# Moving four gate pairs of a hybrid mLSTM/HGRN step between its HGRN heads, parking their sums in DRAM, and another lead-in

## The chip, the cores and the metric

The kernel runs on one core of one Trainium2 chip. The metric is the device time of one execution in microseconds; the time of a kernel is the median of its runs. Everything below is fp32 work; every dense product is carried out as three TensorE passes over parts that are rounded to the fp32r format.

## The reference, cut to what matters

```python
xn = rmsnorm(h, norm_g)
proj = xn @ w_in
u, v_m, z_m, ig, fg, q_h, f_h, i_h, g_h, ga, gb = split(proj)
# branch a: causal conv, 4 mLSTM heads of 512, chunk by chunk
ya = hm @ w_brm
# branch b: 8 HGRN2 heads of 128
lfh = log(lb + (1 - lb) * sigmoid(f_h));  kh = (1 - lb) * sigmoid(-f_h);  qh = silu(q_h)
oh, S_new = hgrn(qh, kh, i_h, lfh, S0)
yb = (head_rmsnorm(oh, hnorm_g) * silu(g_h)) @ w_brh
y = sigmoid(ga) * ya + sigmoid(gb) * yb
h = h + y @ w_out
h = h + sigmoid(h @ w_pg) * (p @ w_ple)
out = rmsnorm(h, final_g)
```

There are 512 prompt frames of a new stream and 32 frames of a running one, a model width of 1024, one layer. The outputs are y for both streams and all new states (conv rows, C, n, m, S). `ga` and `gb` are 1024 wide each, that is 8 units of 128 columns each.

## The kernel before

**Tiles.** The 544 frames lie along the free axis, features along the 128 partitions. A product over 1024 features has 8 slices; for each slice and each half of the frames (272 columns) there are three matmuls: high weight by high x, high weight by low x, low weight by high x. A weight piece of 128x512 comes by DMA into one of 8 raw buffers (`raw_piece`, L122), ScalarE casts it to the high part (L134) and VectorE subtracts to get the low part (L135). So a dense stretch of TensorE has a steady stream of casts, subtractions and PSUM evacuations beside it on ScalarE and VectorE.

**Order.** TensorE's order is written by hand (`tc.manual_schedule`). The other engines run their queues first in, first out; what stands where in them is decided when the program is built, by a priority. In the lead-in (L1392 on) ScalarE and VectorE are also in written order.

**Lead-in.** VectorE sets a tile `warm` to zero (L1396), TensorE runs 8 dummy fp32 matmuls on it (L1399; each shows as two in the trace), then `products(k)` (L1405) for the 8 slices of the first three units. For each slice x is scaled by the norm's gain on ScalarE (L1413, the high part `hi`), VectorE makes its low part (L1414), and the weight piece `wf` is split as above. All loads are issued on SP's queue, x and wf in turn (L205, L124).

**Middle.** Then come the convolution, the four mLSTM heads and the sum over them of `ya` in DRAM (`ya_d`, L1349 to L1360).

**HGRN part.** `units()` (L1692) is a list of pairs of units (`Two`, L479): for each head h the pair (q, f), then (g, i), and after all eight heads four pairs of `ga` and four of `gb` in turn. A pair is computed with seven blocks of 12 matmuls each in place of eight (the sums of weights for it are made by DMA with accumulate and by VectorE), so it takes 14 steps of 6 matmuls. `Pump` (L704) hands these steps to TensorE one by one; `heads()` (L2035) is a generator with the recurrence of the heads: it issues some small TensorE work of a head and what follows it on the other engines, and then yields a number of steps for which the pump runs before the next piece of the chain. These numbers are `GAPS` (L40). The pieces of a head that matter here, by the names of their PSUM tiles:

- `ho` (`output`, L2007): the head's output; then on ScalarE sums of squares, on VectorE a Newton reciprocal root on 128x5 tiles and the scaling of `kq` by it (L2026)
- `hoT` (`finish`, L2098), `GAPS[10]`, `[2]`, `[3]` and `[4]` later, 12 steps in all: transposes of the scaled output back to features by frames; VectorE gates it into `ob` (L2107, L2108)
- `pl` (`scores`): the attention scores of the levels of the recurrence
- `ht` (`columns`, L1819): transposes of `hkq` (the keys) and of `hi` (the values), evacuated by ScalarE (L1822, L1823)
- `su` (`state`, L1988): the state's update from these, `GAPS[8]` steps behind `ht`

`merge_a` (L1747) is run when a `ga` unit is there: sigmoid on ScalarE, `ya` loaded from `ya_d`, VectorE multiplies (L1751), and the product stays in a slot `ya` until the end. `merge_b` (L1754) takes the sigmoid of `gb`. After the last head's `hoT` the pump runs out, with gate pairs alone.

**Seam and end.** Then `p @ w_ple` (tiles `ple`), `yb` (L2194 on): each of the 8 `ob` tiles is split into high and low part (`os`), each unit's 48 matmuls are followed by times `gb`, plus `yas[f]`; then the pairs of `w_out` and `w_pg`, and the final norm.

Of the kernel before, what the change touches and what calls it, by code (L numbers as in the profile page):

```python
# [17 lines left out]
P = 128  # L18
# [9 lines left out]
HH = 8  # L28
# [9 lines left out]
SUB = 5  # L38
LASTS = (0, 3, 6)
GAPS = (2, 2, 1, 3, 6, 2, 4, 2, 2, 4, 2, 8)  # L40
SLOT = 550
NSLOT = 22
NEVAC = 12
# [26 lines left out]
def hybrid_step(ctx: ExitStack, tc: tile.TileContext, a, o):  # L70
# [48 lines left out]
        V.tensor_tensor(lo, src, hi.bitcast(F32), ALU.subtract)  # L119
        return hi, lo  # L120

    def raw_piece(src, name):  # L122
        raw = wp.tile([P, WP], F32, tag="wr", name=name, bufs=NRAW)
        nc.sync.dma_start(raw[:, : src.shape[-1]], src)  # L124
        return raw

    made = {}
# [75 lines left out]
    def load(k):  # L203
        t = eslot(f"x{k}")
        nc.sync.dma_start(t[:, : T + 1], a["xT"][k])  # L205
# [1186 lines left out]

    with tc.manual_schedule(engines={mybir.EngineType.Activation, mybir.EngineType.DVE, mybir.EngineType.PE}):

        warm = small("warm", [P, P], bufs=1, tag="vsm")
        V.memset(warm, 0.0)  # L1396
        wps = paux("warm")
        for _ in range(WARM):
            PE.matmul(wps[:, 0, :P], warm, warm, start=True, stop=True)  # L1399
# [3 lines left out]
        acc.append([u2[:, 0], u2[:, 1]])  # L1403

        def products(k):  # L1405
            for f in range(NF):
                steps(acc[f], wf[k][1:], (k,), f * P, 0)

        for k in range(KD):
            t = xt[k]  # L1410
            hi, lo = pair_tile(f"x0{k}", k // (KD // 2))
            g = t[:, T : T + 1]
            S.mul(hi, t[:, :T], g)  # L1413
            V.scalar_tensor_tensor(lo, t[:, :T], g, hi.bitcast(F32), ALU.mult, ALU.subtract)  # L1414
            x0.append((hi, lo))
            wf[k].append(split_piece(wf[k][0], f"wf{k}", NF * P))
            if k == 1:
                load(KD - 2)
                load(KD - 1)
            sqk = slot(f"r0q{k}")[:, :T]  # L1420
            S.activation(sqk, t[:, :T], AF.Square)
            sq.append(sqk)
            if k in (1, 3):
                V.tensor_tensor(sq[k - 1], sq[k - 1], sqk, ALU.add)
            if k in (5, 6):
                i, j = ((0, 2), (4, 5))[k - 5]
                V.tensor_tensor(sq[i], sq[i], sq[j], ALU.add)
            if k > 1:
                products(k - 2)
# [260 lines left out]
    gbs, yas, gated = [None] * KD, [None] * KD, {}  # L1690

    def units():  # L1692


        def both(h):

            if "both" not in hs[h]:
                t = sp.tile([P, 2, SLOT], F32, tag="d", name=f"hkq{h}", bufs=2)
                hs[h].update(both=(t[:, 0], t[:, 1]), pair=t)
            return hs[h]["both"]  # L1700

        def forget(h, raw):
            lbc, lcc = lb[:, h : h + 1], lc[:, h : h + 1]
            tf, kk = eslot(f"tf{h}"), both(h)[0]
            for t, sign in ((tf, 1.0), (kk, -1.0)):
                S.activation(unrev(t), raw[:, :HB], AF.Sigmoid, scale=sign)
                S.activation(t[:, HB:T], raw[:, HB:T], AF.Sigmoid, scale=sign)
            S.activation(tf[:, :T], tf[:, :T], AF.Identity, scale=lcc, bias=lbc)
            S.mul(kk[:, :T], kk[:, :T], lcc)
            hs[h].update(tf=tf, kk=kk, kq=raw)  # L1710

        def query(h, qq):
            tf, kk, kq = (hs[h][k] for k in ("tf", "kk", "kq"))
            q0 = eslot(f"q0{h}")

            S.activation(unrev(q0), qq[:, :HB], AF.Sigmoid)
            S.activation(q0[:, HB:T], qq[:, HB:T], AF.Sigmoid)
            V.tensor_tensor(unrev(q0), unrev(q0), qq[:, :HB], ALU.mult)
            V.tensor_tensor(q0[:, HB:T], q0[:, HB:T], qq[:, HB:T], ALU.mult)
            V.tensor_tensor(qq[:, :T], q0[:, :T], tf[:, :T], ALU.mult)  # L1720
            hs[h].update(q0=q0, qq=qq)

        def behind(h, then, t):

            if h:
# [12 lines left out]
        def value(h, t):
            hs[h]["ii"] = t

        def gate(h, t):
            sg = slot(f"sg{h}")
            S.activation(sg[:, :T], t[:, :T], AF.Sigmoid)
            V.tensor_tensor(t[:, :T], t[:, :T], sg[:, :T], ALU.mult)
            hs[h]["gg"] = t

        def merge_a(f, t):  # L1747
            gated[f] = S.activation(t[:, :T], t[:, :T], AF.Sigmoid)
            y = slot(f"ya{f}")[:, :T]
            nc.sync.dma_start(y, ya_d[f])  # L1750
            V.tensor_tensor(y, y, t[:, :T], ALU.mult)  # L1751
            yas[f] = y

        def merge_b(f, t):  # L1754
            S.activation(t[:, :T], t[:, :T], AF.Sigmoid)
            gbs[f] = t

        for h in range(HH):
# [22 lines left out]
        for f in range(0, KD, 2):  # L1781
            for e in (
                pair("ga", f, 80 + f, lambda f: plain(eslot(f"ga{f}")), merge_a, True),
                pair("gb", f, 88 + f, lambda f: plain(eslot(f"gb{f}")), merge_b, True),
            ):
                e.alone = True
                yield e

    def triangle(out, x, sign):

# [244 lines left out]
    def heads():  # L2035
# [7 lines left out]
        x.collect()  # L2043
        x.copies(1)
        for h in range(HH):
            yield max(1, pump.when["i", h] - pump.done)
            x.scale(1)
            x.copies(2)
            yield GAPS[1]
            if last:  # L2050
                last.output()
                yield GAPS[10]
            x.values()
            yield GAPS[2]
            x.scale(2)
            x.copies(3)
            x.shares()
            yield GAPS[3]
# [4 lines left out]
            yield GAPS[4]  # L2063
            if last:
                finish(h - 1)
            x.scale(4)
            x.copies(5)
            yield GAPS[5]
            x.scale(5)
            x.copies(6)  # L2070
            nxt = None
            if h + 1 < HH:
                yield max(1, pump.when["q", h + 1] + 1 - pump.done)
                nxt = Head(h + 1)
                nxt.copies(0)
                yield GAPS[6]
            else:
                yield GAPS[11]
# [11 lines left out]
            yield GAPS[7]  # L2090
            x.columns(x.kk, x.kt, x.kts)
            yield GAPS[8]
            x.state()
            last, x = x, nxt
        yield GAPS[9]
        last.output()

    def finish(h):  # L2098
# [14 lines left out]
    with tc.manual_schedule(engines={mybir.EngineType.PE}):  # L2113
# [17 lines left out]
    ps_, ple = [], []  # L2131
    for k in range(2):
        t = slot(f"p{k}")
        nc.sync.dma_start(t[:, :T], a["pT"][k])
        with tc.issue_after(gated[KD // 2 + k].ins):
            ps_.append(split(t[:, :T], f"ps{k}"))

    def ple_units(n, after=None):
        for f in range(len(ple), len(ple) + n):
# [54 lines left out]
    for f in (0, 4, 1, 5, 2, 6, 3, 7):  # L2194
        w = weight(a["w_brh"][f], f"wbh{f}")
        acc = dense(w, 0, P, P, obs, f"yb{f}")
        t = gbs[f]
        for b in range(2):
# [220 lines left out]
```

## Time and profile before

| | us |
|---|---|
| runs: median (lowest to highest of 3) | 1091.33 (1090.9 to 1091.63) |
| the profiled execution, its own time | 1091.98 |
| its span | 1090.0 |
| TensorE busy in it | 1080.7 |
| VectorE busy | 897.3 |
| ScalarE busy | 700.3 |
| GpSimd busy | 217.2 |

A row of the timeline reads: start in us, duration in us, engine, line, operation, output<-inputs by tile name, shape, count; in brackets the idle time before it and what ended it. `PE` is the matmul, `PEld` the load of its weights, which goes ahead of it. Because a matmul's modelled end overlaps the start of the next (0.29 us long, but one starts every 0.125 us), a short wait hardly shows as idle time: it is seen as a larger distance between two starts, and the matmul behind it shows 0.39 in place of 0.29.

### The profile page before, as it was taken

Reading aid. Unit: us, or ns where it says so; the run is one execution under the profiler, and the core shown is the slowest. Engines: PE = TensorE matmul, PEld = TensorE weight load, DVE = VectorE, ACT = ScalarE, POOL = GpSimd, SP = SyncE. Lnnn points to the kernel's source line nnn. Section 1 sums busy time; section 2 is a strip of 40 time slices with the busy share of each in tenths; the row PEclk is TensorE's granted clock in tenths of the full one; section 3 lists DMA queues with packets and bytes.
Section 4 is the critical chain, followed back from the end, with each engine's and each line's share of the span. In section 5 each row is a group of like instructions: output and inputs, shape, how many; then the busy total and the mean of one; then the engine's idle time right before and its main releaser. Section 6 shows DMA issues by size and latency. Waiting matters only on the chain.

```text
span 1090.0 us, 26205 instructions
## 1 busy us (share of the span) xinstructions
PE 1080.7 (99%) x9865; PEld 1054.9 (97%) x9865; DVE 897.3 (82%) x2052; ACT 700.3 (64%) x1619; POOL 217.2 (20%) x399
## 2 busy tenths in 40 slices
PE   9999999999999999999999999999999999999998
PEld 9899999999999999999999999999999999999997
DVE  6889988676897695986888689999999887778886
ACT  7767557754666564765556488778777667446673
POOL 5205010213021122202130033223332210000002
PEclk9999999999999999999999999999999999999999
DMA  6134525648454377555599666667666783327753
GB/s 233 58 117 136 182 66 168 156 136 207 137 170 151 125 169 171 170 171 176 178 257 246 192 147 153 153 145 156 151 155 145 184 224 98 115 89 242 237 195 122
DMA packets 97270, 176.67 MB, mean 162 GB/s; under 512 B 11412, under 2 KB 18580, under 8 KB 96888
## 3 DMA queue, kind: packets, MB, share of 16 engines
q1 hardware_dynamic: 81072, 140.96, 40.1%
q0 software_dynamic: 15184, 32.93, 16.5%
q8 instruction: 77, 1.26, 0.5%
q10 hardware_dynamic: 888, 1.12, 0.3%
q14 instruction: 49, 0.40, 0.1%
HBM read 150.05 MB, written 41.69 MB: 176 GB/s over the span
## 4 chain that ended last, share of the span: by engine, by line
PE 79%; DVE 10%; ACT 6%; DMA 3%; issue 2%; SPq 0%; ACTq 0%; DVEq 0%
PE d L610 33%; PE ya L169 9%; PE yb L169 4%; PE q L169 4%; PE k L169 4%; PE C L1079 4%; PE sc L1039 2%; PE u L293 2%; PE d L462 2%; PE vp L1572 2%; PE nm L1260 2%; DVE hkq L1936 1%; PE ple L169 1%; DMA ws<-in_w_in 1%; DMA kv_d<-vhl 1%
## 5 line engine op out<-in xcount | busy, mean ns | idle before, releaser
L497 POOL DMA_DIRECT2D ws<-in_w_in x46 | 40.3, 883 | 208.8 <-DVE hkq L1936 79.8
L624 ACT COPY t<-d 128x272 f32<-128x272 f32 x153 | 57.9, 378 | 13.6 <-PE d L610 13.4
L1936 DVE TENSOR_TENSOR hkq<-hkq,q 128x288 f32<-128x288 f32 (+1 forms) x96 | 41.8, 437 | 4.4 <-ACT km L1858 3.6
L787 DVE SCALAR_TENSOR_TENSOR cv<-ub,vec,cv 128x547 f32<-128x547 f32 x48 | 37.6, 784 | 1.7 <-ACT cv L782 1.2
L1193 DVE SCALAR_TENSOR_TENSOR c<-c,wi,Cs 128x258 f32<-128x258 f32 x32 | 15.3, 479 | 18.8 <-PE Cs L1191 18.6
L1357 DVE TENSOR_TENSOR y<-ya,y 128x272 f32<-128x272 f32 x48 | 18.9, 435 | 14.3 <-PE ya L169 12.5
L1091 ACT COPY Co<-C 128x258 f32<-128x258 f32 x30 | 9.8, 378 | 27.1 <-PE C L1079 24.8
L779 POOL COPY uo<-ub 128x3 f32<-128x3 f32 x16 | 18.7, 1167 | 34.5 <-DVE ub L633 26.6
L963 POOL COPY ksm<-kf 128x96 f32<-128x96 f32 x16 | 8.1, 510 | 84.8 <-ACT kf L977 84.8
L135 POOL TENSOR_TENSOR wple50l<-wple5r,wple50h 128x256 fp32r<-128x256 f32 x1 | 0.7, 737 | 120.1 <-ACT wple50h L134 120.1
L1271 ACT COPY y<-nm 128x516 f32<-128x516 f32 x16 | 9.5, 591 | 23.0 <-PE nm L1260 22.5
L963 POOL COPY vsm<-vt 128x96 f32<-128x96 f32 x12 | 6.3, 526 | 85.9 <-ACT vt L635 43.5
L1248 DVE BATCH_NORM_STATS2 bs<-y 128x6 f32<-128x512 f32 (+1 forms) x20 | 13.8, 691 | 8.1 <-ACT y L1271 7.8
L583 POOL DMA_DIRECT2D ws<-in_w_in x14 | 14.3, 1023 | 29.8 <-DVE ws272l L135 26.6
L1260 PE MATMUL nm<-vhl,sh 128*128 128x258 f32 x112 | 18.4, 286 | 0.0
L378 POOL DMA_DIRECT2D w_pg_d<-in_w_pg x16 | 13.1, 820 | 25.3 <-issue 22.1
L1977 POOL COPY at<-at 32x128 f32<-32x128 f32 x32 | 17.9, 558 | 1.4 <-ACT at L1958 0.4
L2022 ACT ACTIVATE kit<-kq 128x128 f32<-128x128 f32 x32 | 9.7, 304 | 12.0 <-DVE kq L2018 12.0
L1008 DVE TENSOR_TENSOR ql<-q,qh 128x272 fp32r<-128x272 f32 x24 | 9.4, 434 | 8.3 <-ACT qh L1007 7.2
L378 POOL DMA_DIRECT2D w_out_d<-in_w_out x16 | 13.5, 1005 | 12.7 <-issue 10.6
L1260 PEld LDWEIGHTS nm<-vhl,sh 128*128 128x128 f32 x112 | 15.5, 190 | 0.6 <-ACT Co L1091 0.5
L1792 POOL TENSOR_SCALAR_AFFINE_SELECT aa<-at 128x128 f32<-128x128 f32 x32 | 15.7, 523 | 0.6
(4748 smaller groups left out, 5112.5 us busy)
## 6 DMA issues: line engine op xcount, KB each, us to landing
ws<-in_w_in POOLq DMA_DIRECT2D x60, 256.0 KB, 5.1
ws<-in_w_in SPq DMA_DIRECT2D x46, 256.0 KB, 4.0
ya_d<-y SPq DMA_DIRECT2D x32, 272.0 KB, 2.3
y<-ya_d SPq DMA_DIRECT2D x24, 272.0 KB, 3.6
w_out_d<-in_w_out POOLq DMA_DIRECT2D x24, 256.0 KB, 6.2
w_pg_d<-in_w_pg POOLq DMA_DIRECT2D x24, 256.0 KB, 6.3
c<-in_C SPq DMA_DIRECT2D x16, 258.0 KB, 3.6
out_Cs<-c SPq DMA_DIRECT2D x16, 258.0 KB, 3.7
```

Of the source, the lines that this page charges most:

```text
L169: PE.matmul(both[b][:m, :TH], part(w, off + k * step, m, x), xx[:, half(b)], start=(k == 0 and j == 0), stop=(k == n - 1 and j == 2),)
L293: PE.matmul(both[b][:m, :TH], part(w, off + k * step, m, x), xx[:, half(b)], start=(k == 0 and j == 0), stop=(k == KD - 1 and j == 2),)
L378: G.dma_start(late[g][n][k], src, accum_op=ALU.add)
L462: PE.matmul(self.ps[b][:, : c.stop - c.start], part(self.w, k * P, P, x), xx[:, c], start=(k == 0 and j == 0), stop=(k == KD - 1 and j == 2),)
L497: G.dma_start(t, piece(u, i), accum_op=ALU.add)
L610: PE.matmul(ps, ww[:, c], xx, start=(start and k == 0 and j == 0), stop=end, skip_group_check=not start,)
L624: self.kept = S.copy(t, ps)
L787: V.scalar_tensor_tensor(cv[:, :547], ub[:, j : j + 547], vcol(V_CW + 4 * ft + j), cv[:, :547], ALU.mult, ALU.add)
L1039: PE.matmul(pn[:, 0, :n], ks[f][x][:, j * P : (j + 1) * P], qs[f][y][:, NS + j * P : T], start=(f == 0 and i == 0), stop=(f == KH - 1 and ...
L1079: PE.matmul(pn[g][:, :VH], kw[b][x][:, f * P : (f + 1) * P], vv[b][y][:, g * VH : (g + 1) * VH], start=(b == 0 and j == 0), stop=(b == NB ...
L1260: PE.matmul(pn[:, g, :VH], st[j][x][:, (i - j) * P : (i - j + 1) * P], vv[j][y][:, g * VH : (g + 1) * VH], start=(j == 0 and q == 0), stop ...
L1936: V.tensor_tensor(x, x, d, ALU.mult)
```

## The change

Four parts.

1. **Lead-in.** The dummy matmuls take a constant zero as operand, so that nothing is set by VectorE before them. The first two pieces of `wf` are loaded on ScalarE's queue. For slice 0 VectorE casts the weight, ScalarE scales x in two halves, VectorE makes the low parts by halves, and the low part of the weight comes last; the 18 matmuls of slice 0 go pass by pass over the three units, not unit by unit.
2. **Gate pairs.** The four `ga` pairs are yielded behind heads h = 3, 4, 5, 6 (`SPREAD`), the four `gb` pairs behind head 7.
3. **Gaps.** Heads 3 to 6 take `WIDE`, the last head `LAST`; the last `hoT` follows 14 steps after the chain's end (`LASTGAP`), not 16, which now falls right ahead of the seam.
4. **Parked sums.** `merge_a` stores the product of gate and `ya` back to `ya_d`; the loop over `yb` loads it again as `yg`, two tiles before the first weight and then one unit ahead. The two splits of p are made within the first two `gb` units that are in `PSAT`.

```diff
+LAST = (2, 4, 2, 4, 8, 4, 4, 2, 2, 4, 4, 8)
+WIDE = (2, 4, 4, 6, 8, 4, 4, 2, 2, 4, 4, 8)
+SPREAD = (3, 4, 5, 6)
+LASTGAP = 14
...
-        wf.append([raw_piece(a["w_first"][k], f"wf{k}r")])
+        wf.append([raw_piece(a["w_first"][k], f"wf{k}r", nc.scalar if k < 2 else nc.sync)])
...
-        warm = small("warm", [P, P], bufs=1, tag="vsm")
-        V.memset(warm, 0.0)
+        warm = nc.const_aps.tensor(0.0, [P, P], F32)
...
+            for j, (x, xx) in enumerate(((0, x0[0][0]), (0, x0[0][1]), (1, x0[0][0]))):
+                for f in range(NF):
+                    for b in range(2):
+                        PE.matmul(
...
+                V.tensor_copy(wh, wf[0][0][:, : NF * P])
+                for b in range(2):
+                    S.mul(hi[:, half(b)], t[:, half(b)], g)
...
+                V.tensor_tensor(wl, wf[0][0][:, : NF * P], wh.bitcast(F32), ALU.subtract)
...
             V.tensor_tensor(y, y, t[:, :T], ALU.mult)
-            yas[f] = y
+            nc.sync.dma_start(ya_d[f], y)
...
+            if h in SPREAD:
+                yield next(gates)
+        yield from gates
...
+            gaps = WIDE if h in SPREAD else LAST if h == HH - 1 else GAPS
...
-        pump.to(pump.done + 16)
+        pump.to(pump.done + LASTGAP)
...
+        for g in order[:2] if i == 0 else order[i + 1 : i + 2]:
+            yas[g] = slot(f"yg{g}")[:, :T]
+            nc.sync.dma_start(yas[g], ya_d[g])
```

**How the order moves.** First the lead-in on TensorE, from its first matmul, before (`u0*`, `u1*`, `u2` are the halves of the three units, `x00` is x's slice 0, `wf0h` and `wf0l` the weight's parts):

```order
L1399 MATMUL warm_152<-warm_150 128x128 x8
L293 MATMUL u00_161<-x00_167,wf0h_170 128x272
L293 MATMUL u01_162<-x00_167,wf0h_170 128x272
L293 MATMUL u00_161<-x00_167,wf0h_170 128x272
L293 MATMUL u01_162<-x00_167,wf0h_170 128x272
L293 MATMUL u00_161<-x00_167,wf0l_171 128x272
L293 MATMUL u01_162<-x00_167,wf0l_171 128x272
```

and the same place of the changed kernel:

```order
L1403 MATMUL warm_150<-const-float32-0.0 128x128 x8
L1417 MATMUL u00_159<-x00_165,wf0wh_166 128x272
L1417 MATMUL u01_160<-x00_165,wf0wh_166 128x272
L1417 MATMUL u10_161<-x00_165,wf0wh_166 128x272
L1417 MATMUL u11_162<-x00_165,wf0wh_166 128x272
L1417 MATMUL u2_164<-x00_165,wf0wh_166 128x272 x2
```

The low part of the weight is now first used by the thirteenth matmul, not by the fifth.

The second place is the transposes `hoT` of head 3, on TensorE, before (`wa2253` and `ws453` are weights of pairs' blocks, `d` their PSUM tiles):

```order
L610 MATMUL d530_11102<-xfh3_1326,wa2253h_11304 128x272
L610 MATMUL d530_11102<-xfl3_1327,wa2253h_11304 128x272
L610 MATMUL d530_11102<-xfh3_1326,wa2253l_11305 128x272
L2103 MATMUL hoT3_11442<-anti_123,kq3_10023 128x128 x2
L2103 MATMUL hoT3_11442<-ident_104,kq3_10023 128x128 x2
L2104 MATMUL hoT3_11442<-anti_123,osb_10419 128x128
L610 MATMUL d531_11103<-xh4_886,ws453h_11371 128x272
```

and of the changed kernel:

```order
L615 MATMUL d771_11676<-xh7_912,wa1277h_11634 128x272
L615 MATMUL d771_11676<-xl7_913,wa1277h_11634 128x272
L615 MATMUL d771_11676<-xh7_912,wa1277l_11635 128x272
L2142 MATMUL hoT3_11722<-anti_123,kq3_10023 128x128 x2
L2142 MATMUL hoT3_11722<-ident_104,kq3_10023 128x128 x2
L2143 MATMUL hoT3_11722<-anti_123,osb_10419 128x128
L615 MATMUL d530_11468<-xfh0_1308,wa2253h_11652 128x272
```

`hoT` stands one block earlier in the pair of unit 53, but the blocks of the gate pair lie ahead of it: counted in the two orders, there are 72 dense matmuls between this head's `ho` and its `hoT` before, and 132 now; between `hoT` and the first matmul on the next weight `ws277`, 12 before and 24 now. Between `ht` of the keys and `su` there are 12 in both; between the scores ahead of it and `ht`, 12 in both.

The third place is VectorE's queue at the seam, in the changed kernel (`wbh` are weights of `yb`, `os` low parts of the `ob` tiles, `ob7` the last head's output):

```order
L140 TENSOR_TENSOR wbh00l_14247<-wbh0r0_14242,wbh00h_14246 128x512
L636 TENSOR_TENSOR gb6_13961<-d941_13960,t1694_14097 128x272
L2146 SCALAR_TENSOR_TENSOR ob7_14164<-hoT7_14158,vec_78,hg7_13059 128x512
L2147 SCALAR_TENSOR_TENSOR ob7_14164<-hoT7_14158,vec_78,hg7_13059 128x32
L124 TENSOR_TENSOR os3_14177<-ob3_11728,os3_14177 128x544
L124 TENSOR_TENSOR os4_14180<-ob4_12419,os4_14180 128x544
L124 TENSOR_TENSOR os5_14183<-ob5_13110,os5_14183 128x544
L124 TENSOR_TENSOR os6_14186<-ob6_13742,os6_14186 128x544
L124 TENSOR_TENSOR os7_14189<-ob7_14164,os7_14189 128x544
L140 TENSOR_TENSOR wbh01l_14251<-wbh0r512_14244,wbh01h_14250 128x512
```

Before, the two `ob7` rows stood some 55 rows ahead of `wbh00l`; all else of these rows was there in nearly the same sequence. On SP's queue 14 DMAs come in on balance (8 stores and 8 loads of 272 KB added, 2 weight loads gone to ScalarE's queue); the number of TensorE instructions is the same but for one row that is printed apart.

More of the change, by code (lines that the diff above doesn't have):

```diff
@@ L120, in psplit, with raw_piece @@
         return hi, lo
-    def raw_piece(src, name):
+    def raw_piece(src, name, queue=None):
         raw = wp.tile([P, WP], F32, tag="wr", name=name, bufs=NRAW)
-        nc.sync.dma_start(raw[:, : src.shape[-1]], src)
+        (queue or nc.sync).dma_start(raw[:, : src.shape[-1]], src)
         return raw
@@ L1405, in products @@
         def products(k):
-            for f in range(NF):
-                steps(acc[f], wf[k][1:], (k,), f * P, 0)
+            if k:
+                for f in range(NF):
+                    steps(acc[f], wf[k][1:], (k,), f * P, 0)
+                return
+            for j, (x, xx) in enumerate(((0, x0[0][0]), (0, x0[0][1]), (1, x0[0][0]))):
+                for f in range(NF):
+                    for b in range(2):
+                        PE.matmul(
+                            acc[f][b][:, :TH],
+                            part(wf[0][1:], f * P, P, x),
+                            xx[:, half(b)],
+                            start=(j == 0),
+                            stop=False,
+                        )
         for k in range(KD):
@@ L1412, in hybrid_step @@
             g = t[:, T : T + 1]
-            S.mul(hi, t[:, :T], g)
-            V.scalar_tensor_tensor(lo, t[:, :T], g, hi.bitcast(F32), ALU.mult, ALU.subtract)
             x0.append((hi, lo))
-            wf[k].append(split_piece(wf[k][0], f"wf{k}", NF * P))
+            if k:
+                S.mul(hi, t[:, :T], g)
+                V.scalar_tensor_tensor(lo, t[:, :T], g, hi.bitcast(F32), ALU.mult, ALU.subtract)
+                wf[k].append(split_piece(wf[k][0], f"wf{k}", NF * P))
+            else:
+                first = [wp.tile([P, WP], F32R, tag=tag, name=f"wf0{tag}") for tag in ("wh", "wl")]
+                wh, wl = (x[:, : NF * P] for x in first)
+                V.tensor_copy(wh, wf[0][0][:, : NF * P])
+                for b in range(2):
+                    S.mul(hi[:, half(b)], t[:, half(b)], g)
+                    V.scalar_tensor_tensor(
+                        lo[:, half(b)], t[:, half(b)], g, hi[:, half(b)].bitcast(F32), ALU.mult, ALU.subtract
+                    )
+                V.tensor_tensor(wl, wf[0][0][:, : NF * P], wh.bitcast(F32), ALU.subtract)
+                wf[0].append(first)
             if k == 1:
@@ L1751, in merge_a, with gate_pairs @@
             V.tensor_tensor(y, y, t[:, :T], ALU.mult)
-            yas[f] = y
+            nc.sync.dma_start(ya_d[f], y)
         def merge_b(f, t):
-            S.activation(t[:, :T], t[:, :T], AF.Sigmoid)
+            opened = S.activation(t[:, :T], t[:, :T], AF.Sigmoid)
             gbs[f] = t
+            if f in PSAT:
+                k = len(ps_)
+                x = slot(f"p{k}")
+                nc.sync.dma_start(x[:, :T], a["pT"][k])
+                with tc.issue_after(opened.ins):
+                    ps_.append(split(x[:, :T], f"ps{k}"))
+        def gate_pairs():
+            for what, unit, then in (("ga", 80, merge_a), ("gb", 88, merge_b)):
+                for f in range(0, KD, 2):
+                    e = pair(what, f, unit + f, lambda f, what=what: plain(eslot(f"{what}{f}")), then, True)
+                    e.alone = True
+                    yield e
+        gates = gate_pairs()
         for h in range(HH):
@@ L1780, in units @@
             )
[L1781 to L1787, printed above, removed]
+            if h in SPREAD:
+                yield next(gates)
+        yield from gates
     def triangle(out, x, sign):
@@ L2048, in heads @@
             x.copies(2)
-            yield GAPS[1]
+            yield gaps[1]
             if last:
                 last.output()
-                yield GAPS[10]
+                yield gaps[10]
             x.values()
-            yield GAPS[2]
+            yield gaps[2]
             x.scale(2)
@@ L2057, in heads @@
             x.shares()
-            yield GAPS[3]
+            yield gaps[3]
             x.scores(paux(f"pl{h}8")[:, 0])
@@ L2062, in heads @@
             x.copies(4)
-            yield GAPS[4]
+            yield gaps[4]
             if last:
@@ L2067, in heads @@
             x.copies(5)
-            yield GAPS[5]
+            yield gaps[5]
             x.scale(5)
@@ L2075, in heads @@
                 nxt.copies(0)
-                yield GAPS[6]
+                yield gaps[6]
             else:
-                yield GAPS[11]
+                yield gaps[11]
             pn = paux(f"pl{h}64")
@@ L2089, in heads @@
                 nxt.copies(1)
-            yield GAPS[7]
+            yield gaps[7]
             x.columns(x.kk, x.kt, x.kts)
-            yield GAPS[8]
+            yield gaps[8]
             x.state()
             last, x = x, nxt
-        yield GAPS[9]
+        yield LAST[9]
         last.output()
@@ L2124, in hybrid_step @@
         pump.run(heads())
-        pump.to(pump.done + 16)
+        pump.to(pump.done + LASTGAP)
         finish(HH - 1)
         pump.end()
[L2131 to L2136, printed above, removed]
+    ple = []
     def ple_units(n, after=None):
@@ L2192, in h_sums @@
         hf[k] = half_sums(f"h{k}", h1[k], h1[k + HK], h1s[k], h, l, h6, l6, after)
-    for f in (0, 4, 1, 5, 2, 6, 3, 7):
-        w = weight(a["w_brh"][f], f"wbh{f}")
+    order = (0, 4, 1, 5, 2, 6, 3, 7)
+    for i, f in enumerate(order):
+        for g in order[:2] if i == 0 else order[i + 1 : i + 2]:
+            yas[g] = slot(f"yg{g}")[:, :T]
+            nc.sync.dma_start(yas[g], ya_d[g])
+        with tc.issue_after(pump.todo[-1].kept.ins) if i == 0 else nullcontext():
+            w = weight(a["w_brh"][f], f"wbh{f}")
         acc = dense(w, 0, P, P, obs, f"yb{f}")
```

5 lines of the change are left out of this document (3 added, 2 removed).

## The prediction

> **What bounds the kernel now.** I read the page first (busy time by engine), then the busy time by stretch where the change works, then what the weight loads of TensorE waited for there, then the timeline around each wait.
>
> ```profile
> PE 1080.7 (99%) x9865; PEld 1054.9 (97%) x9865; DVE 897.3 (82%) x2052; ACT 700.3 (64%) x1619; POOL 217.2 (20%) x399
> ...
> 715.00:831.00 116.00, 114.99 (x1600) 110.60 (x1599) 105.67 (x307) 90.04 (x264) 36.79 (x63) 1.00 0.67 148
> ...
> 858.00:926.00 68.00, 68.00 (x543) 67.70 (x542) 52.82 (x104) 45.36 (x98) 9.15 (x14) 1.00 0.61 162
> ```
>
> TensorE (first figure behind the length of a stretch) is the bound everywhere, so only its waits can be won. VectorE (the third) is at 105.67/116 = 91% while heads run, and at 78% where gate pairs run alone. The change mixes the two kinds of work. The waits of the stretch 715 to 930:
>
> ```profile
> PEld ht L1819 <- DVE hkq L1936: 1.3, 5, 0.3
> PEld hoT L2103 <- PE d L610: 1.1, 3, 0.4
> PEld su L1988 <- ACT kit L1823: 0.6, 2, 0.4
> PEld d L610 <- DVE ws276l L135: 0.4, 1, 0.4
> PEld d L610 <- DVE ws288l L135: 0.4, 1, 0.4
> PEld d L610 <- ACT t L624: 0.2, 1, 0.2
> ```
>
> Columns: total us, times, longest. (A row of 1.5 us that names no releaser is left out.) This is 4.0 us, 0.37% of the kernel, and that is nearly all that the moved pairs can bring.
>
> **Gate pairs and gaps: `hoT`.** An undisturbed transpose follows the last dense matmul by 0.15 us, a waiting one by 0.45:
>
> ```profile
> 726.23 0.29 PE L610 MATMUL d<-xfh,wa2252l 128*128 128x272 f32 x1
> 726.38 0.41 PE L2103 MATMUL hoT<-anti,kq 128*128 128x128 f32 x2
> ...
> 755.60 0.29 PE L610 MATMUL d<-xfh,wa2253l 128*128 128x272 f32 x1
> 756.05 0.41 PE L2103 MATMUL hoT<-anti,kq 128*128 128x128 f32 x2 [0.17 <-DVE kq L2026]
> ```
>
> ```profile
> 755.23 0.68 DVE L2026 TENSOR_TENSOR kq<-kq,hr 128x512 f32<-128x512 f32 x1
> ```
>
> So the releaser is `kq` on VectorE, which ends at 755.9, and the row "PE d" in the table above names only what stood ahead. It happens three times (heads 3 to 5), 0.45 - 0.15 = 0.30 at this one, 1.1 us by the table. There are 72 dense matmuls from `ho` to `hoT`; the chain misses this by 0.3 us. The change makes them 132. At 0.125 us each (below) that is 7.5 us more, against an added VectorE load of one gate pair, of which by the last stretch (78%) about 8 us fall in 10.5 us and only a part in this window. I take the whole 1.1 us, at least half of it.
>
> **Behind `hoT`.** VectorE gates the transposes into `ob`, and then only makes the low part of the next weight:
>
> ```profile
> 756.99 0.74 DVE L2107 SCALAR_TENSOR_TENSOR ob<-hoT,vec,hg 128x512 f32<-128x512 f32 x1
> 757.65 0.68 DVE L135 TENSOR_TENSOR ws277l<-ws,ws277h 128x512 fp32r<-128x512 f32 x1
> ```
>
> ```profile
> 728.62 0.29 PE L610 MATMUL d<-xfl,ws276h 128*128 128x272 f32 x1
> 729.06 0.39 PE L610 MATMUL d<-xfh,ws276l 128*128 128x272 f32 x1 [0.15 <-DVE ws276l L135]
> ...
> 758.39 0.39 PE L610 MATMUL d<-xfh,ws277l 128*128 128x272 f32 x1
> 758.62 0.29 PE L610 MATMUL d<-xfh,ws277h 128*128 128x272 f32 x1
> ```
>
> At 729.06 the matmul starts 0.44 behind its neighbour instead of 0.13. At 758.39 the weight was there by a hair (757.65 + 0.68 = 758.33), and still the next start is 0.23 later, not 0.13: a near miss costs 0.10, and shows in no table. Between `hoT` and this weight there will be 24 matmuls, not 12, 1.5 us more than a wait of 0.31. The rows `ws276l` and `ws288l` go: 0.8 us, and some four near misses of 0.1, that is 0.3 to 0.4. I take 1.1 us; the low end is 0.4, one of the two.
>
> **`su` and `ht`.** Both stand as far behind their sources as before (12 matmuls), so nothing in the order frees them.
>
> ```profile
> 826.14 0.25 ACT L1823 COPY kit<-ht 32x128 f32<-32x128 f32 x1
> ```
>
> ```profile
> 825.96 0.29 PE L610 MATMUL d<-xh,wa1280l 128*128 128x272 f32 x1
> 826.44 0.82 PE L1988 MATMUL su<-hi,hkq 128*128 128x128 f32 x5 [0.19 <-ACT kit L1823]
> ```
>
> `su` waited for ScalarE's queue, in two of five heads, so it hangs on what else stands in it. I take half of 0.6. `ht` waits in all five, for VectorE's `hkq`; I take it as staying, with ends at 1.3 won and 0.3 lost. Where a pair moved in, other pieces may turn late (the PSUM copies of the gate pair stand in ScalarE's and VectorE's queues between links of a chain): ends 0 and 1.2 us, and I take 0.3, one wait of the common size for the four heads together.
>
> **Parked sums.** Eight stores and eight loads, 272 KB each; the same transfer in the old direction:
>
> ```profile
> ya<-ya_d SPq DMA_DIRECT2D x8, 272.0 KB, 5.7
> ```
>
> A load lands 5.7 us after issue; `yg` is wanted only behind 48 matmuls of `yb` (6 us) and then once per 6 us. 4.4 MB more over some 200 us are 22 GB/s on top of 148 to 162 in the rows of stretches. Both cost nothing: TensorE's dense work hides them. A store on SP's queue has to wait for VectorE's product, and weight pieces are queued behind it. What covers it is how early these are issued, here the two pieces of unit 90:
>
> ```profile
> L124 SPq DMA_DIRECT2D wi90r<-in_w_in x2: 327/328/328, 829.8 to 832.1; - x2
> L134 ACT CAST wa1190h<-wi90r x1: 613/613/613, 857.4 to 857.4; 128x512 fp32r<-128x512 f32 x1
> ```
>
> They are issued at 829.8 and 832.1, and the first is cast at 857.4, 27 us later. Without that cover each us of delay would be one us of TensorE. Low end 0, high end 0.5.
>
> **The seam.** The last `hoT` now stands 20 `ple` matmuls ahead of `yb`, so `ob7` and its split come into the row of work there.
>
> ```profile
> 922.87 0.39 ACT L635 ACTIVATE gb<-d 128x272 f32<-128x272 f32 x1
> ...
> 928.09 0.64 ACT L134 CAST wbh01h<-wbh0r 128x512 fp32r<-128x512 f32 x1
> ```
>
> ```profile
> 921.90 2.65 DVE L119 TENSOR_TENSOR os<-ob,os 128x544 fp32r<-128x544 f32 x4 [0.50 <-ACT os L118]
> ...
> 928.98 0.69 DVE L135 TENSOR_TENSOR wbh01l<-wbh0r,wbh01h 128x512 fp32r<-128x512 f32 x1
> ```
>
> ScalarE goes from the last `gb` to `wbh01h` in 928.73 - 922.87 = 5.9 us, with the same rows in both orders. TensorE comes to `wbh01h` behind 5 transposes (0.6 us), 20 and 24 matmuls (5.5 us): 6.1 us. VectorE gets `ob7` in addition, 0.74 us by the row behind `hoT` above and a little more for the sample columns, and the end of the last head's root chain ahead of it. The chain has 76 matmuls, 9.5 us, where 72 missed by 0.3 under heavier load. I charge 0.3 us (ends 0 and 2.0).
>
> **The lead-in.**
>
> ```profile
> 0.80 0.39 SPq L205 DMA_DIRECT2D x<-in_xT  x1
> ...
> 1.12 3.78 PE L1399 MATMUL warm<-warm 128*128 128x128 f32 x16 [1.12 <-DVE emc L1242]
> ...
> 3.53 0.75 ACT L1413 ACTIVATE x<-x 128x544 fp32r<-128x544 f32 x1 [1.44 <-DMA x<-in_xT]
> ...
> 4.18 0.49 ACT L134 CAST wf0h<-wf0r 128x384 fp32r<-128x384 f32 x1
> ...
> 5.01 0.55 DVE L135 TENSOR_TENSOR wf0l<-wf0r,wf0h 128x384 fp32r<-128x384 f32 x1
> ```
>
> ```profile
> 4.73 1.28 PE L293 MATMUL u<-x,wf0h 128*128 128x272 f32 x4
> 5.80 0.66 PE L293 MATMUL u<-x,wf0l 128*128 128x272 f32 x2
> 6.25 1.05 PE L293 MATMUL u<-x,wf0h 128*128 128x272 f32 x4
> 7.14 0.42 PE L293 MATMUL u<-x,wf0l 128*128 128x272 f32 x2
> 7.39 0.66 PE L293 MATMUL u<-x,wf0h 128*128 128x272 f32 x4
> ```
>
> The dummies wait for VectorE until 1.12; an engine that waits for nothing starts at 0.80. They may start 0.3 us earlier and end by about 4.45. x is there at 3.53, half of it scaled by 3.9 (half of 0.75); the weight's cast on VectorE, which the trace doesn't show, lies between ScalarE's 0.49 and VectorE's 0.55 for the shape, so 4.1 to 4.7 by where the piece lands. First useful matmul: 4.5 for 4.73. Matmuls start (7.14 - 5.80)/6 = 0.223 apart until about 7.0, and (7.39 - 7.14)/2 = 0.125 behind it. An earlier start is worth 1 - 0.125/0.223 = 0.44 less than itself: 0.23 x 0.56 = 0.13 us. If the fast step also comes 0.3 earlier, 0.3 x 0.44 = 0.13 more. I take 0.2 us, ends 0 and 0.3.
>
> [...]
>
> **The sum**, against the profiled execution: -1.1 (`hoT`) - 1.1 (weights behind it) - 0.3 (`su`) + 0.3 (new waits) + 0.3 (seam) - 0.2 (lead-in) = -2.1 us. 1091.98 - 2.1 = 1089.9; the profiled run stands 0.65 over the median of 1091.33, so the median is forecast at **1089.2 us**.
>
> **Rivals.**
> - *Everything late goes* (chance 0.12): the mix puts VectorE at (105.67 + 4 x 8.2)/(116 + 42) = 88% instead of 91%, with 0.78 x 10.5 = 8.2 us for a gate pair, and `ht` and `su` are freed too. -1.1 - 1.1 - 0.6 - 1.3 - 0.3 = -4.4 at most, some -3.5 as a middle: 1087.8. Against it: the distance to `ht` is the same.
> - *Waits move on* (0.25): the chains are freed at `hoT` but a gate pair's copies hold up `ho`, `ht` or `su`, 1.2 us, and only half of the behind-`hoT` gain comes: 1090.7. For it: 88% is still close to full.
> - *Clock step* (0.06): the step from 0.223 to 0.125 could come at another time in the changed kernel, for reasons of its phase. The median moves by 0.44 us per us of it: with 3 us, 1090.5 or 1087.9. Against it: three runs lie within 0.73 us. [...]
> - *Slower at the seam* (0.09): between `hoT` and the first use of `wbh01l` TensorE has 20 + 28 matmuls, 6.0 us; VectorE has about 0.4 for a `gb` half, 0.9 for `ob7`, 5 x 2.65/4 = 3.3 for the splits and 0.7 for `wbh01l`, 5.3. From a backlog of 0.7 us on, each us more is a us of TensorE. Without the seam's 0.3 the forecast is 1088.9; the gain is eaten at a backlog of 0.7 + 2.4 = 3.1 us, and at 5.3 us the time is 1093.5, over 0.2% slower. Against it: VectorE sat idle several times at this seam before.
>
> The forecast has 0.48. From the ends of its terms it covers about 1088.2 to 1090.3.
>
> **Chances.** A measurement of this kernel tells about 0.2% from no change, 1089.15 to 1093.5. The forecast lies on that edge: half of its 0.48, the first rival's 0.12 and most of the clock rival's better half, plus the favourable end of the terms, make faster 0.43; slower 0.08; the rest, 0.49, is same. The range leaves out one in ten at each side: 1087.6, the middle of the first rival, to 1091.8, half way up the seam.
>
> **What would show it.** In the changed profile: no row of `hoT` among the waits of heads 4 to 7; no 0.39 us matmul on the weight behind `hoT`; `ht` rows as before; the first useful matmul at or before 4.6. It is wrong if a wait for `ho`, for `wbh01l`, or for a weight's DMA of over 1 us stands in the table, or if VectorE in the widened heads stays over 91%.

## The result

The changed kernel takes 1099.40 us (median of 4 runs, 1098.32 to 1101.13) against 1091.21 for the kernel before (1090.90 to 1091.63): ratio 1.0076, 95% interval 1.0059 to 1.0094. It is slower by 8.2 us where 2.1 us of gain were forecast. One slow run, of 1309.02 us in the fourth experiment, is left out of the figures below. The profiled execution took 1101.13 us, with a span of 1099.3, 9.3 more than before.

Of the page, the span and the busy times. Every engine's busy time stands within 4.3 us of before, TensorE's within 1.7, so most of the new time is waiting:

```profile
span 1099.3 us, 26227 instructions
PE 1082.4 (98%) x9865; PEld 1055.7 (96%) x9865; DVE 901.1 (82%) x2053; ACT 702.1 (64%) x1619; POOL 212.9 (19%) x399
```

Of the busy time by stretch, the one from 715 to 900 us, first before, then after (the length, then TensorE's busy time and matmul records, its weight loads, VectorE, ScalarE, GpSimd, granted clock, DMA share, GB/s). TensorE got 126 matmul records less done in the same time (46 of them come in the next 30 us, where the chain of a later head now stands); its busy time in all stretches up to 715 agrees within 0.2 us:

```profile
715.00:900.00 185.00, 183.84 (x2265) 178.68 (x2264) 165.00 (x448) 137.45 (x381) 50.87 (x83) 1.00 0.69 166
```

```profile
715.00:900.00 185.00, 176.40 (x2139) 171.07 (x2138) 158.19 (x415) 132.13 (x358) 45.55 (x74) 0.99 0.73 174
```

What the weight loads of TensorE waited for after the change, from 715 to 930 us (us in all, times, longest); before, the same view had 1.3 for `ht`, 0.6 for `su` and 0.2 for `t`:

```profile
PEld ht L1857 <- DVE hkq L1974: 7.8, 10, 2.1
PEld d L615 <- ACT t L629: 4.5, 7, 1.3
PEld su L2026 <- ACT hkq L1860: 1.2, 3, 0.4
```

The rows of `hoT`, `ws276l` and `ws288l` are gone, as forecast. In their place stand waits for `t`, the PSUM copies of ScalarE, and for `hkq` of VectorE's recurrence, up to 2.1 us each. The timeline of ScalarE, VectorE and TensorE around the first of them shows what holds these up:

```profile
731.78 0.40 ACT L1896 COPY km<-hkq 128x256 f32<-128x256 f32 x1
735.45 0.62 ACT L139 CAST ws452h<-ws 128x512 fp32r<-128x512 f32 x1 [3.27 <-DMA ws<-in_w_in]
735.98 0.61 ACT L139 CAST ws176h<-ws 128x512 fp32r<-128x512 f32 x1
736.50 0.38 ACT L629 COPY t<-d 128x272 f32<-128x272 f32 x1
```

```profile
736.11 0.69 DVE L140 TENSOR_TENSOR ws452l<-ws,ws452h 128x512 fp32r<-128x512 f32 x1 [3.43 <-ACT ws452h L139]
```

```profile
735.61 0.27 PE L2143 MATMUL hoT<-anti,osb 128*128 128x128 f32 x1
736.93 0.39 PE L615 MATMUL d<-xfh,wa2252h 128*128 128x272 f32 x1 [1.04 <-ACT t L629]
```

ScalarE is done with `km` at 732.2, and the next in its queue is the cast of `ws452`. This is the last of a pair's weight sums; it is made by adding a piece of `w_in` in place by an accumulating DMA (L588), which hasn't landed. ScalarE stands for 3.3 us, and VectorE, whose next in line is the low part of the same weight, for 3.4. `ws452` itself isn't wanted by TensorE until 738.6; what TensorE misses is `t`, the copy behind the cast in the queue. The same a little later, where the recurrence (`hkq`) stands behind the low part of `ws476`, a weight that TensorE wants at 757:

```profile
747.78 0.62 ACT L139 CAST ws476h<-ws 128x512 fp32r<-128x512 f32 x1 [2.23 <-DMA ws<-in_w_in]
```

```profile
748.43 0.69 DVE L140 TENSOR_TENSOR ws476l<-ws,ws476h 128x512 fp32r<-128x512 f32 x1 [1.92 <-ACT ws476h L139]
749.04 0.42 DVE L1974 TENSOR_TENSOR hkq<-hkq,q 128x256 f32<-128x256 f32 x1
```

```profile
747.60 0.28 PE L615 MATMUL d<-xh,wa1182l 128*128 128x272 f32 x1
749.52 0.44 PE L1857 MATMUL ht<-ident,hkq 128*128 128x128 f32 x2 [1.63 <-DVE hkq L1974]
...
751.13 0.43 PE L615 MATMUL d<-xl,wa1182h 128*128 128x272 f32 x1
751.36 0.43 PE L615 MATMUL d<-xh,wa1182l 128*128 128x272 f32 x1
```

Before the change, `hkq` stood ahead of that low part in VectorE's queue:

```profile
735.36 0.42 DVE L1936 TENSOR_TENSOR hkq<-hkq,q 128x256 f32<-128x256 f32 x1
...
738.39 0.68 DVE L135 TENSOR_TENSOR ws476l<-ws,ws476h 128x512 fp32r<-128x512 f32 x1
```

Ten rows lie between the two, and `ht` (735.84) needs `hkq` alone. Now the order is turned round, and it is so for all four weights `ws476` to `ws479`. Of the 13.5 us in the three rows of TensorE's waits, 8.2 come within 5 us behind the casts of these four.

Behind the wait of 749.52 the matmuls start 0.23 us apart for 3 us, and the granted clock (the figure behind GpSimd's) is 0.50 there:

```profile
750.20:753.40 3.20, 3.19 (x14) 3.20 (x15) 3.20 (x12) 2.57 (x9) 2.56 (x7) 0.50 0.83 160
```

Fourteen matmuls at 0.10 us too much are 1.4 us more. With 13.5 us of waits in the three rows against 4.0 in all rows of before this is a growth of 10.9. Against it stand 0.5 us by which the lead-in of this trace was shorter (below) and the rows for `pl`, left out in both, which fell from 1.5 to 0.7: 9.6, and the span grew by 9.3.

ScalarE's waits from 715 to 900 us that the view puts down to these DMAs:

```profile
ACT ws455h L139 <- DMA ws<-in_w_in: 4.3, 1, 4.3
ACT ws452h L139 <- DMA ws<-in_w_in: 3.3, 1, 3.3
ACT ws454h L139 <- DMA ws<-in_w_in: 2.8, 1, 2.8
ACT ws478h L139 <- DMA ws<-in_w_in: 2.4, 1, 2.4
ACT ws476h L139 <- DMA ws<-in_w_in: 2.2, 1, 2.2
ACT ws453h L139 <- DMA ws<-in_w_in: 1.8, 1, 1.8
ACT ws479h L139 <- DMA ws<-in_w_in: 1.3, 1, 1.3
```

An eighth, `ws477h`, waited 1.2 us. The view names TensorE's `pl` for it, but its own DMA, issued at 783.08, landed 5.80 us later, just ahead of the cast at 788.96.

Before the change the casts of `ws452` to `ws455` had no wait at all. That of `ws452` in the timeline of before, with the issue of its DMA on GpSimd's queue, 8.3 us ahead:

```profile
713.95 1.24 POOL L583 DMA_DIRECT2D ws<-in_w_in  x1
```

```profile
722.22 0.60 ACT L134 CAST ws452h<-ws 128x512 fp32r<-128x512 f32 x1
```

After the change the issue is at 727.72, and the cast would have been reached 4.5 us later:

```profile
727.72 1.22 POOL L588 DMA_DIRECT2D ws<-in_w_in  x1
```

The casts of `ws476` to `ws479` waited for 1.0, 1.2, 1.5 and 1.7 us before (the first two are put down to `d`, but their DMAs landed 0.1 us ahead of them), not much less than the 2.2, 1.2, 2.4 and 1.3 now. That cost TensorE little, since `hkq` didn't stand behind them.

### The profile page after: what moved, and what is told of

The parts are those of the page before. It is cut to its first block, busy times and chain, and to the rows that moved or that the text cites. A ratio compares the mean times of both kernels' runs of the same rounds, so it can differ in the third digit from the quotient of the medians.

```text
span 1099.3 us, 26227 instructions
## 1 busy us (share of the span) xinstructions
PE 1082.4 (98%) x9865; PEld 1055.7 (96%) x9865; DVE 901.1 (82%) x2053; ACT 702.1 (64%) x1619; POOL 212.9 (19%) x399
## 4 chain that ended last, share of the span: by engine, by line
PE 73%; DVE 12%; DMA 6%; ACT 5%; issue 2%; SPq 0%; POOL 0%; DVEq 0%; ACTq 0%
PE d L615 28%; PE ya L174 9%; PE q L174 4%; PE yb L174 4%; PE k L174 4%; PE C L1084 4%; DMA ws<-in_w_in 4%; PE nm L1265 3%; PE sc L1044 2%; PE d L467 2%; PE vp L1600 2%; PE u L298 2%; DVE hkq L1974 2%; DVE ws L576 1%; PE ple L174 1%
## 5 line engine op out<-in xcount | busy, mean ns | idle before, releaser
L588 POOL DMA_DIRECT2D ws<-in_w_in x14 | 14.7, 1051 | 28.6 <-DVE ws272l L140 27.0
L2015 POOL COPY at<-at 32x128 f32<-32x128 f32 x32 | 14.7, 459 | 23.6 <-ACT at L1996 22.6
L383 POOL DMA_DIRECT2D w_out_d<-in_w_out x16 | 13.5, 1006 | 14.8 <-issue 12.8
L1058 ACT CAST sh<-dm 128x512 fp32r<-128x512 f32 (+3 forms) x16 | 7.2, 457 | 12.9 <-DVE dm L1052 12.9
L1084 PE MATMUL C<-vhl,kwh 128*128 128x258 f32 x96 | 15.4, 283 | 0.0
```

Source lines behind the costliest of these rows:

```text
L383: G.dma_start(late[g][n][k], src, accum_op=ALU.add)
L1084: PE.matmul(pn[g][:, :VH], kw[b][x][:, f * P : (f + 1) * P], vv[b][y][:, g * VH : (g + 1) * VH], start=(b == 0 and j == 0), stop=(b == NB ...
```

## The experiments

Twelve kernels; each is timed beside the kernel before on the same chip, whose median was 1091.4 to 1091.7 there.

**Lead-in alone.** The kernel of before with the lead-in of the change (part 1 of the change, nothing else).

> The kernel of before with the changed lead-in alone. If the 8 us sit in the heads with gate pairs, as the trace of the changed kernel reads, this is within 0.5 us of before, by the prediction's term 0.2 us faster (1091.0). If the lead-in had a share in the loss, it is slower than 1091.8.

Measured: 1091.45 us, ratio 0.9997 (0.9988 to 1.0007). The lead-in has no share in the loss.

**The last weight sum on VectorE.** In the changed kernel the pairs of the later heads are treated like the gate pairs: the last sum is made by VectorE from a raw piece, with no accumulating DMA for it.

```diff
-            first.alone = h == 1
+            first.alone = h == 1 or h > 3
...
-            yield Two(
+            second = Two(
...
+            second.alone = h > 2
+            yield second
```

> The changed kernel, with the last weight sum of every pair of heads 3 or 4 and later added on VectorE from the raw piece (as the gate pairs do it) and no longer by an accumulating DMA on GpSimd's queue. Theory A (the accumulating DMA lands late, the cast that waits for it stands at the head of ScalarE's queue, and the PSUM copies and recurrence copies behind it make TensorE wait): the casts of ws452, ws476, ws454 and so on no longer wait for a DMA, and most of the loss goes, to 1090 to 1093 us. Theory B (VectorE and ScalarE simply have too much to do in the widened heads, so the recurrence is late): VectorE has 0.68 us more for each of some 9 pairs, and the time stays at 1098 or goes above it. Theory C (transfers of ya): no change, 1098 to 1100.

Measured: 1087.15 us (1086.66 to 1087.46), ratio 0.9958 (0.9943 to 0.9972): the loss is gone, and the gain that the change was to bring shows, which is more than expected. None of the other kernels here is faster than this one by more than the noise. Theory A holds. B falls, as VectorE has more to do here (171.9 us busy from 715 to 900 against 158.2) and the time still falls; C falls, as the transfers of `ya` are the same. From 715 to 900 us nothing is left of the waits but this (a first row without a releaser aside):

```profile
PEld d L615 <- ACT t L629: 0.4, 1, 0.4
PEld pl L1925 <- PE d L615: 0.2, 1, 0.2
```

**No parking.** The changed kernel without store and reload of the gated sums (`yas[f] = y` again, the loop's loads out).

> The changed kernel without parking: merge_a keeps its product in its slot until the seam, with no store and no reload. Theory C1 (the eight stores delay SP's queue and the accumulating DMAs): 2 to 5 us of the loss go, 1094 to 1097 us. Theory A with another cause of the lateness (the loads of ya and of the gate pair's weights ahead in SP's queue): 1098 to 1100, as the changed kernel.

Measured: 1102.39 us (1097.77 to 1103.87), ratio 1.0090 (1.0067 to 1.0114), above either expectation. Parking doesn't cause the loss.

**No traffic of ya at all.** `merge_a` takes the sigmoid only; the product with `ya` is left out of y.

> The changed kernel, where merge_a takes the sigmoid alone: no load of ya, no product with the gate, no store (the branch's gate is left out of y). Theory C (the transfers of ya, 272 KB each, make the weight sums late): the loss goes, 1090 to 1093 us. If the gate pair's own place is enough to make them late, it stays above 1096. VectorE also has 1.5 us less for each gate pair, by which theory B would win 1 to 3 us.

Measured: 1093.22 to 1098.82 us in five runs, ratio 1.0047 (1.0031 to 1.0064). That is some 2 to 3 us better than the change, at the edge of the noise, as fewer VectorE instructions and transfers may bring. The casts still wait (`ws452h` 3.5 us, `ws479h` 3.3): the gate pairs' place and gaps are enough.

**The VectorE sum without the change.** The kernel of before with the edit of the second experiment.

> The kernel of before with the same edit as the second run (the last weight sum of the pairs of heads 3 or 4 and later made on VectorE). If that edit is good by itself, whatever the change, this is 1087 to 1089 us too. If it only mends what the change broke, this stays at 1090.5 to 1092.5: the casts on ScalarE waited for accumulating DMAs by 1.7 us at most before, and TensorE hardly for them; VectorE's 91% would rise to some 95%.

Measured: 1091.28 us, ratio 0.9999 (0.9990 to 1.0008). That edit is worth nothing by itself; it mends what the change broke, and the 4 us of the second experiment belong to the change.

**Old gaps, VectorE sum.** The second experiment with `GAPS` for heads 3 to 6:

```diff
-            gaps = WIDE if h in SPREAD else LAST if h == HH - 1 else GAPS
+            gaps = LAST if h == HH - 1 else GAPS
```

> The second run (changed kernel, last weight sum on VectorE) with the old gaps for heads 3 to 6 in place of the wide ones; the last head keeps its own. If the wide gaps hide the output's and the transposes' waits, as the prediction has it, their rows come back: three or four waits of 0.3 before hoT and the weights behind it, 1088.5 to 1090. If the gate pairs' place is what helps, 1087.2 as the second run.

Measured: 1091.76 us, ratio 1.0001 (0.9992 to 1.0011). Without the wide gaps the gain is gone, which is a larger loss than expected. Rows of `hoT` were expected; what comes is waits for weights whose subtraction stands behind the gating `ob` in a VectorE queue without idle time:

```profile
PEld d L615 <- DVE ws254l L140: 1.0, 1, 1.0
PEld d L615 <- DVE ws252l L140: 0.9, 1, 0.9
PEld d L615 <- DVE ws253l L140: 0.7, 1, 0.7
```

**VectorE sum for all heads.** The second experiment with `first.alone = h > 0` and `second.alone = True`.

> The second run with the last weight sum on VectorE for the pairs of all heads but the first two units (q, f) of head 0. The waits of 0.3 on ws274l and ws275l between 669 and 699 us stand behind an accumulating DMA that is late by 0.1 to 0.6 us; if those DMAs cause them, 1086 to 1087. If VectorE at 88 to 91% there becomes late with 0.68 us more for each pair, 1088 to 1090.

Measured: 1087.13 us, ratio 0.9959 (0.9944 to 0.9973), the same as the second. `ws274l` and `ws275l` still cost 0.4 and 0.3 us, so the DMA wasn't their cause; that guess falls.

**The cast later in the queue.** The changed kernel with all its DMAs; the casts of the last sums, from head 3 on, are only written two blocks later into the program.

```diff
+                if make and i == 6 and isinstance(e, Two) and e.early and not e.alone and not e.made and n > 5:
+                    self.held.append((self.made + 2, make))
+                    make = None
+                while self.held and self.held[0][0] <= self.made:
...
+                        held(self.raw)
```

> The changed kernel with the accumulating DMAs left as they are, but the casts that wait for them written two blocks later into the program, so that PSUM copies and copies of the recurrence stand ahead of them in ScalarE's queue. Theory A1 (the loss is what stands behind the cast in ScalarE's queue; the weight itself is not late for TensorE): most of the loss goes, 1090 to 1094, and ScalarE's waits for these DMAs fall under 1 us each. Theory A2 (the weight is late for TensorE itself, or VectorE's queue behind the subtraction is what counts): 1097 or more, with waits of TensorE for ws452l and its like.

Measured: 1091.00 us (1089.66 to 1092.45), ratio 0.9993 (0.9984 to 1.0003). By the medians 8.4 us of the change's time go by the place of these casts in ScalarE's queue, and of the subtractions behind them in VectorE's, with the transfers untouched. The edit moves both places at once, so it doesn't tell their shares. Its timeline of ScalarE: the cast of `ws452` now stands behind the next `hkq`, and has no wait:

```profile
735.06 0.42 ACT L1745 ACTIVATE hkq<-kq 128x256 f32<-128x256 f32 x1
735.39 0.60 ACT L139 CAST ws452h<-ws 128x512 fp32r<-128x512 f32 x1
735.90 0.38 ACT L629 COPY t<-d 128x272 f32<-128x272 f32 x1
```

What keeps it from 1087 are other waits from 620 to 930 us, 1.9 us for `su` and 1.6 and 0.8 for the weights `ws475l` and `ws451l`, whose casts were held back too.

**Old gaps, accumulating DMA.** The changed kernel with the gaps of the sixth experiment.

> The changed kernel with the old gaps for heads 3 to 6, the weight sums by accumulating DMA as they are. If the wide gaps are what lets ScalarE come to the waiting casts too early (less of the recurrence stands between the cast of one sum and that of the next), the waits of ScalarE for these DMAs shrink and this is 1091 to 1094, as with the sums on VectorE and the old gaps (1091.8). If the gate pairs' place alone makes the DMAs late, it is 1097 or more.

Measured: 1121.84 us, ratio 1.0271 (1.0252 to 1.0290). My guess that the wide gaps cause the early casts was wrong in sign: they soften them. ScalarE waits up to 5.4 us here, and TensorE 13.0 us for `ht` and 9.5 for `t` from 715 to 900, with a granted clock of 0.96 from 720 to 900:

```profile
ACT ws452h L139 <- DMA ws<-in_w_in: 5.4, 1, 5.4
ACT ws479h L139 <- DMA ws<-in_w_in: 5.0, 1, 5.0
```

So I counted in the traces what stands in ScalarE's queue between the cast of the pair's sum `ws2` and that of `ws4`, since the accumulating DMA can start only when `ws2` is split. For the pairs (q, f) of heads 5 to 7 (units 53 to 55):

| | rows of ScalarE between the two casts | from the end of `ws2`'s split to where ScalarE reaches `ws4`'s cast, us | to where it starts, us |
|---|---|---|---|
| before | 29 | 8.9 | 8.9 |
| changed | 10 | 4.9 | 6.7 to 9.2 |
| changed, old gaps | 8 | 3.0 | 7.3 to 8.0 |
| changed, casts held | 17 | 9.4 | 9.4 |

The DMAs land 5 to 8 us behind their issue in all of them (5.2 to 7.0 before from 700 on, 5.7 to 7.9 after from 715 on). What the change moved for these pairs is the chain: with a gate pair between, the copies of the values' transposes `ht` and the scalings behind them, which stood between these two casts, now run while other blocks are on TensorE. With less in between, ScalarE comes to the second cast before its data.

The count doesn't explain the other waits. For `ws452` it is 15 rows and 7.6 us, and there GpSimd issued the DMA only 3.1 us behind the split (0.7 before). For the pairs (g, i), `ws476` to `ws479`, it is 13 or 14 rows before and 14 after, and ScalarE comes to the cast 4.9 to 5.1 us behind the split before, 5.5 to 6.1 after, so later and not earlier. What turned there is VectorE's order, with `ws476l` ahead of `hkq` (above).

**No parking, VectorE sum.** The second experiment with the third's edit.

> The second run (changed kernel, last weight sum on VectorE) without parking: the gated sums stay in their slots, no store, no reload. If parking costs nothing by itself, 1087.2 within 0.5. If the slots that it frees are needed, slower than 1088.5; if its 16 transfers cost, faster than 1086.5.

Measured: 1087.45 us, ratio 0.9960 (0.9946 to 0.9975). Parking costs nothing and brings nothing here.

**Old lead-in, VectorE sum.**

> The second run with the old lead-in. The first slice's matmuls end 0.46 us earlier in the changed lead-in by the traces, so 1087.6 is expected; if the lead-in is worth nothing, 1087.2.

Measured: 1087.34 us, ratio 0.9963 (0.9950 to 0.9976). The lead-in can't be told from nothing, again.

**Gate pairs behind six heads.** The seventh experiment with `SPREAD = (1, 2, 3, 4, 5, 6)`.

> The seventh run (last weight sums on VectorE for all heads) with gate pairs behind heads 1 to 6, six of them, and the wide gaps there. The waits of heads 0 to 2 that are left (some 2 us between 620 and 715, near misses included) would go as those of heads 3 to 6 did: 1085.5 to 1086.5. If the gb tiles that now live longer take buffers from the heads, or the seam gets more work at a time, 1088 or more.

Measured: 1089.03 us, ratio 0.9978 (0.9969 to 0.9988), 1.9 us worse than with four. Of the waits from 614 to 715 us 1.0 are left of the seventh experiment's 2.8, but the gain that was expected from them is more than eaten. One wait of a new kind shows, 1.2 us of `ho` for GpSimd's `aa`, and behind it one of 0.9 us of the last `hoT`. From 900 to 930 TensorE is busy for 28.07 us against 29.88 in the seventh experiment, which is nearly the whole loss.

## Why the prediction was wrong, step by step

- **What bounds the kernel**: right in that TensorE's waits alone decide, and wrong in reading TensorE's waits as the only ones that matter. ScalarE's own waits already had the casts of `ws476` to `ws479` at 1.0 to 1.7 us for a DMA, harmless where they stood.
- **`hoT` and the weights behind it, -2.2**: the mechanism was right. The rows of `hoT`, `ws276l` and `ws288l`, 1.9 us, are gone in the changed kernel and with the queue mended (second experiment). There `ht` is down from 1.3 to 0.3 and `su` from 0.6 to nothing as well, which the sum had at 0 and 0.3, and the change's heads are worth some 4 us (1087.15 against 1091.28 to 1091.7). That is the size of the first rival, -4.4 at most, but not for its reason: VectorE wasn't less loaded there (171.9 us of 185, 93%, against 165.0 or 89% before). The wide gaps are needed for the gain (sixth experiment, 4.6 us).
- **New waits, +0.3, with ends 0 and 1.2**: this is the step that failed. The rows of `ht`, `su` and `t` grew from 2.1 to 13.5 us, and 1.4 us of lowered clock came with them. I looked for copies that stand in the way, but not for rows in the queue that wait for a transfer. The eighth experiment shows that this was it: with these casts later in the queue, 8.4 us go. The order showed it beforehand, for the pairs (q, f) with 29 rows between two casts before and 10 after, against a DMA of 5 to 7 us.
- **`ht`, taken as staying, with ends 1.3 won and 0.3 lost**: failed with it, and it is the larger part; the row went from 1.3 to 7.8 us. "Nothing in the order frees them" counted the 12 matmuls of TensorE between source and use. In VectorE's queue, where `hkq` is made, the subtraction of a weight that waits for a DMA had come ahead of it.
- **The sign of a weight's DMA**: the prediction named a wait of over 1 us for one as a sign of being wrong, but only in TensorE's table. It stood in ScalarE's, up to 4.3 us.
- **The range**: its lower end, 1087.6, is called the middle of the first rival, which the text has at 1087.8. Nothing hangs on it.
- **Parked sums, 0**: right (third and tenth experiments).
- **The seam, +0.3**: right, no wait of over 0.5 us stands there. The rival that ended slower was put at the seam, with VectorE's backlog; the loss sat in the heads, in the queues of ScalarE and VectorE.
- **The lead-in, -0.2**: can't be told from nothing (first and eleventh experiments), so it is neither confirmed nor refuted. The timeline shows the terms otherwise:

```profile
4.04 0.94 ACT L1439 ACTIVATE x<-x 128x272 fp32r<-128x272 f32 x2 [1.03 <-DMA x<-in_xT]
4.21 0.37 DVE L1437 CAST wf0wh<-wf0r 128x384 fp32r<-128x384 f32 x1 [3.14 <-DMA wf0r<-in_w_first]
...
4.73 2.37 PE L1417 MATMUL u<-x,wf0wh 128*128 128x272 f32 x12
6.93 0.91 PE L1417 MATMUL u<-x,wf0wl 128*128 128x272 f32 x6
7.68 0.67 PE L298 MATMUL u<-x,wf1h 128*128 128x272 f32 x4
```

x is scaled from 4.04 on, not 3.53. SP issues its DMA at 0.80 in both traces; before, it lands 2.7 us later, and now ScalarE still waits for it until 4.04, 3.2 us behind the issue. Two things are new beside this transfer: the first weight piece is issued on ScalarE's queue at 0.80 too, where it was issued behind x at 1.25 on SP's, and two more slices of x follow the first directly on SP's queue. No run takes one of them alone, so which of them delays x by 0.5 us isn't shown. The first useful matmul stands at 4.73 as before, not at 4.5; in the traces of the first and second experiments, which have the new lead-in, it stands at 4.84 and 4.93. The weight's cast on VectorE took 0.37 us, less than the 0.49 to 0.55 of the estimate, but started only at 4.21.

The second slice still begins at 7.68 instead of 8.14. The first 12 matmuls take 6.93 - 4.73 = 2.20 us, where the slow step of 0.223 would make 2.68, so the fast step came earlier in this trace. That isn't the change's doing: with the same new lead-in the second slice begins at 9.34 and 9.39 in the traces of the sixth and ninth experiments, and with the old one at 7.63 in that of the eleventh. With the new lead-in it begins at 7.59 and 7.58 in those of the first and second. So the step's time differs from run to run, as the clock rival had it, and the 0.5 us of this trace are luck. That rival's 3 us are shown by no run: the starts with the new lead-in that are named here lie 1.8 us apart at most.

## What to carry to other kernels

Where engines run their queues first in, first out, an instruction that waits for a DMA holds up everything behind it (here the cast of `ws452` on ScalarE, 3.3 us, with the copy `t` behind it, for which TensorE then stood 1.0 us), and its own lateness is not the price: list, for every instruction that reads a transfer, how much work stands between what starts the transfer and it, in the order of before and of after. Moving a chain of work away from between the two shortens that distance, though no instruction of the pair itself is touched. Look on every engine for the turned order, too: a row that waits for a transfer may have come ahead of a link of the chain. And a gain that is overlaid by such a loss is seen only with the loss taken out, here by one flag for the pairs.

## What the runs showed of the hardware that was not expected

A wait of TensorE of 1.8 us (747.60 to 749.52, where starts are 0.13 apart else) was followed by a granted clock of 0.50 for 3.4 us, which cost some 1.4 us more. Waits of 1.0 us (736.93) were not. But neither was a longer one in the same trace, 830.72 to 832.84. The two differ in how they lie in time. In the trace of the change the granted clock falls to 0.50 twice: from 750.09 to 753.51, and, behind the last matmul, from 1098.25 to the end. The two starts are 348.16 us apart, 102 times 3.413. On a grid of that step through them (stretch, TensorE's busy time and records, granted clock, DMA share, GB/s) the first wait lies in one piece and the second is cut in two at 832.01:

```profile
746.68:750.09 3.41, 1.64 (x12) 1.00 0.34 99
750.09:753.51 3.42, 3.30 (x15) 0.50 0.83 158
828.60:832.01 3.41, 2.40 (x82) 1.00 0.80 174
832.01:835.42 3.41, 2.33 (x17) 1.00 0.82 160
```

The piece from 746.68 on has 1.77 us of idle TensorE, more than any other between 6 us and the last matmul, and is the only one of these behind which the clock stood at 0.50. The two pieces of the second wait have 1.01 and 1.08 us, and full clock behind them. In the trace of before, where the longest wait of a weight load from 715 to 930 us was 0.4, no 0.50 stands between 8 and 1089 us. No experiment was made for this; it is read off one trace with one such piece, with modelled ends of matmuls, and that the cut at 832.01 spared the second wait is an estimate from it. In the ninth experiment, where weight loads waited up to 4.6 us, the mean clock of 0.96 over 180 us is by itself an estimated 7 us of loss (0.04 x 180).
